# A mixture of softmaxes on one core: units go through TensorE in pairs, and a pair's whole rows are stored at once

## The chip, the core and the metric

The kernel runs on one core of one Trainium2 chip. The metric is the time of one execution on the device in microseconds (us). Before the change it is 789.89 us, the median of three runs (789.84 to 789.98). From here on a time is in us unless it is marked ns, and MB in the working means 1,048,576 bytes where a DMA of 1 MB or 4 MB is meant (the profile's own byte counts are in millions).

## The reference

For each of 32 x 128 = 4096 rows there are four heads with 4096 logits each, and four prior values. The result is a mixture of the four softmaxes, weighed by the softmax of the prior:

```python
prior_probs = softmax(prior, axis=-1)        # (32, 128, 4)
softmax     = softmax(logits, axis=-1)       # (32, 128, 4, 4096)
mixture     = np.sum(prior_probs[..., None] * softmax, axis=2)   # (32, 128, 4096)
```

All of it is float32. The logits are 268 MB, the result is 67 MB; each is moved once.

## The kernel before

**Units and slots.** The 4096 rows make 32 groups `g` of 128 rows, a group is two halves `j` (every second row), and one half with its four heads is a *unit*: 64 rows x 4 heads x 4096 values, 4 MB. There are N = 64 units. A unit lies on 128 partitions as (row m, q): partition 2m + q holds two heads of row m (`i` = 0, 1), 16 KB each, so 32 KB per partition. Five such buffers (`slots`) go round. `load` (L66 to L72) is one DMA of 4 MB on SyncE's queue, and the load of a later unit is issued when the last matmul that reads the slot's present unit is done.

**A unit's work.** For each of the two heads `i` of a partition, `top(n, i)` (L74) takes the negated maximum on VectorE (one 128 x 4096 reduction, L76) and the exponential in place on ScalarE, which also leaves the sum (L79). `weigh(n, i)` (L83) takes the reciprocal of the sum on VectorE (L84), builds a 128 x 64 weight matrix on GpSimd (L86: the selection matrix `sel` times the reciprocal times the prior's share), and issues eight matmuls on TensorE (L93). They sum over the 128 partitions, so that out of (m, q) come 64 rows. The array is used as two column tiles of 64: tile c = 0 makes the columns 0 to 2047 of the 64 rows on PSUM partitions 0 to 63, tile c = 1 the columns 2048 to 4095 on partitions 64 to 127, both with the same weights. The pass with i = 0 starts the sums, the pass with i = 1 adds to them.

**PSUM and the way out.** A unit fills one of two accumulators `accs` (128 x 2048 float32, four banks each), in turn. `evict(n)` (L113) is one ScalarE copy of 128 x 2048 from PSUM to `obuf`, in which group g has one of two halves of 16 KB per partition. When both units of a group are there, `store(g)` (L115) issues two DMAs of 1 MB on ScalarE's queue (L101): one from partitions 0 to 63, one from partitions 64 to 127, each with 8 KB runs, half a row each.

**Order.** The order is written out by hand. In iteration n (w = n - 1 is the unit before) the engines get: `top(n, 0)`; `weigh(w, 1)`, then the load that takes over w's slot; `top(n, 1)`; `weigh(n, 0)`; `evict(w)`; and the store, if w ends a group. So VectorE takes the reciprocal of `weigh(w, 1)` only after the first reduction of unit n, and ScalarE copies w out only after both exponentials of unit n. An engine runs its instructions in this order, and so a waiting instruction holds up what stands behind it.

**End.** The stores of the groups from `HOLD` = 26 to 29 (units 52 to 59, 8 MB) are held back until all loads are issued, so that TensorE, VectorE and ScalarE can finish the last units beside them. Groups 26 and 27 wait in `obuf`, groups 28 and 29 in slot 4, which is no longer loaded, and groups 30 and 31 go to another free slot. The last unit is loaded, copied out and stored in halves.

Of the kernel before, what the change touches and what calls it, by code (L numbers as in the profile page):

```python
# [9 lines left out]
ALU = mybir.AluOpType  # L10
# [3 lines left out]
M = 64  # L14
J = 2
Q = 2
BANK = 512
SLOTS = 5


@with_exitstack
def kernel(
    ctx: ExitStack,
    tc: tile.TileContext,
    logits: bass.AP,
    prior: bass.AP,
    out: bass.AP,
):
    nc = tc.nc
    B, S, H, V = logits.shape  # L30
    R = M * J
    G = B * S // R
    N = G * J
    W = V // 2
    assert G * R == B * S and G == 32 and H == 2 * Q and V == 8 * BANK


    lg = logits.rearrange("b s h v -> (b s) h v").rearrange(
        "(g m j) (q i) v -> g j m q (i v)", m=M, j=J, i=Q
    )  # L40
    ov = out.rearrange("b s v -> (b s) v").rearrange("(g m j) v -> g m j v", m=M, j=J)
    pv = prior.rearrange("b s h -> (b s) h").rearrange("(g r) h -> g r h", r=R)

    cpool = ctx.enter_context(tc.tile_pool(name="cpool", bufs=1))
    psum = ctx.enter_context(tc.tile_pool(name="psum", bufs=1, space=bass.MemoryType.PSUM))

    slots = [cpool.tile([P, Q, V], FP32, name=f"slot{i}") for i in range(SLOTS)]

    obuf = cpool.tile([P, J, V], FP32, name="obuf")
    accs = [psum.tile([P, W], FP32, name=f"acc{i}") for i in range(2)]  # L50

    sel = cpool.tile([P, M], FP32, name="sel")
    wts = [[cpool.tile([P, M], FP32, name=f"wt{k}{i}") for i in range(Q)] for k in range(2)]
    pr = cpool.tile([G, R, H], FP32, name="pr")
    pn = cpool.tile([G, J, Q, M, Q], FP32, name="pn")
    pmax = cpool.tile([G, R], FP32, name="pmax")
    pp = cpool.tile([P, J, Q, G], FP32, name="pp")
    nmax = [cpool.tile([P, N], FP32, name=f"nmax{i}") for i in range(Q)]
    dsum = [cpool.tile([P, N], FP32, name=f"dsum{i}") for i in range(Q)]
    rden = [cpool.tile([P, N], FP32, name=f"rden{i}") for i in range(Q)]  # L60


    def slot(n):
        return slots[n % SLOTS if n < N - 5 else (n - N + 5) % 4]

    def load(n):  # L66
        src = lg[n // J, n % J]
        for i in range(0, Q, Q if n < N - 1 else 1):
            k = Q if n < N - 1 else 1
            nc.sync.dma_start(  # L70
                out=slot(n)[:, i : i + k], in_=src[:, :, i * V : (i + k) * V]
            )  # L72

    def top(n, i):  # L74
        x = slot(n)[:, i]
        nc.vector.tensor_reduce(  # L76
            out=nmax[i][:, n : n + 1], in_=x, axis=AX.X, op=ALU.max, negate=True
        )
        nc.scalar.activation(  # L79
            x, x, AF.Exp, bias=nmax[i][:, n : n + 1], accum_out=dsum[i][:, n : n + 1]  # L80
        )

    def weigh(n, i):  # L83
        nc.vector.reciprocal(rden[i][:, n : n + 1], dsum[i][:, n : n + 1])  # L84
        wt = wts[n % 2][i]
        nc.gpsimd.tensor_scalar(  # L86
            out=wt, in0=sel, scalar1=rden[i][:, n : n + 1],
            scalar2=pp[:, n % J, i, n // J : n // J + 1], op0=ALU.mult, op1=ALU.mult,
        )

        for b in range(W // BANK):
            for c in range(2):
                nc.tensor.matmul(  # L93
                    accs[n % 2][c * M : (c + 1) * M, b * BANK : (b + 1) * BANK],
                    lhsT=wt,
                    rhs=slot(n)[:, i, c * W + b * BANK : c * W + (b + 1) * BANK],
                    start=i == 0, stop=i == Q - 1,
                )

    def part(eng, g, c, js=slice(0, J), lo=0, hi=W):  # L100
        eng.dma_start(  # L101
            out=ov[g, :, js, c * W + lo : c * W + hi],
            in_=home(g)[c * M : (c + 1) * M, js, lo:hi],
        )

    HOLD = G - 6

    def home(g):
        x = obuf if g < G - 4 else slots[4] if g < G - 2 else slot(N - 4)
        return x[:, g % 2].rearrange("p (j w) -> p j w", j=J)  # L110

    def evict(n, lo=0, hi=W):
        nc.scalar.copy(home(n // J)[:, n % J, lo:hi], accs[n % 2][:, lo:hi])  # L113

    def store(g):  # L115
        for c in range(2):
            part(nc.scalar, g, c)

    def prior_user(n):
        return max(k for k in range(n) if slot(k) is slot(n))  # L120

    with tc.manual_schedule():
        for n in range(SLOTS):
            load(n)
        nc.scalar.dma_start(out=pr, in_=pv)

        nc.gpsimd.memset(sel, 1.0)  # L127
        nc.gpsimd.affine_select(  # L128
            out=sel, in_=sel, compare_op=ALU.is_ge, fill=0.0, base=0,
            pattern=[[-Q, M]], channel_multiplier=1,  # L130
        )
        nc.gpsimd.affine_select(  # L132
            out=sel, in_=sel, compare_op=ALU.is_ge, fill=0.0, base=Q - 1,
            pattern=[[Q, M]], channel_multiplier=-1,
        )

        nc.vector.reduce_max(pmax, pr, axis=AX.X)  # L137
        nc.vector.tensor_sub(pr, pr, pmax.unsqueeze(2).to_broadcast([G, R, H]))  # L138
        nc.scalar.activation(pr, pr, AF.Exp)  # L139
        nc.vector.reduce_sum(pmax, pr, axis=AX.X)  # L140
        nc.vector.reciprocal(pmax, pmax)  # L141
        prv = pr.rearrange("g (m j) (q i) -> g j i m q", j=J, i=Q)
        pmv = pmax.rearrange("g (m j) -> g j m", j=J)
        for j in range(J):
            for i in range(Q):
                nc.vector.tensor_mul(  # L146
                    pn[:, j, i], prv[:, j, i], pmv[:, j].unsqueeze(2).to_broadcast([G, M, Q])
                )
        pq = pn.rearrange("g j i m q -> g j i (m q)")
        for t in range(P // 32):  # L150
            nc.vector.transpose(  # L151
                pp[32 * t : 32 * (t + 1)], pq[:, :, :, 32 * t : 32 * (t + 1)]
            )

        for n in range(N):
            w = n - 1
            top(n, 0)
            if n == N - 2:
                for g in range(HOLD, G - 2):
                    part(nc.scalar, g, 1)  # L160
            if w >= 0:
                weigh(w, 1)
                for k in range(SLOTS, N):
                    if prior_user(k) == w:
                        load(k)
                if w == N - 3:
                    for g in range(HOLD, G - 2):
                        part(nc.sync, g, 0)
            top(n, 1)
            weigh(n, 0)  # L170
            if w >= 0:
                evict(w)
                g = w // J
                if w % J == J - 1 and g < HOLD:
                    store(g)
                elif w == N - 3 or w == N - 2:
                    js = slice(0, J) if w == N - 3 else slice(0, 1)
                    part(nc.sync, g, 0, js)
                    part(nc.scalar, g, 1, js)

        n = N - 1
        weigh(n, 1)
        for lo in (0, W // 2):
            evict(n, lo, lo + W // 2)
            part(nc.sync, n // J, 0, slice(1, 2), lo, lo + W // 2)
            part(nc.scalar, n // J, 1, slice(1, 2), lo, lo + W // 2)
# [30 lines left out]
```

## Time and profile before

| what | value |
|---|---|
| median of three runs | 789.89 |
| the profiled execution | 789.42 |
| its span | 787.7 |
| time around the span | 1.7 |
| busy: VectorE / ScalarE / TensorE matmul / GpSimd | 573.4 / 599.8 / 539.4 / 51.1 |
| VectorE reductions, 128 of 128 x 4096 | 4410 ns each |
| ScalarE exponentials, 128 of 128 x 4096 | 3708 ns each, and 187 ns to read the sum |
| ScalarE copies out of PSUM, 56 of 128 x 2048 to `obuf` | 1844 ns each |
| mean granted TensorE clock | 0.88 |

A busy share below 80% on every engine says that none of them sets the time by its sum alone. The matmul row is the time in which at least one matmul was in the array, and it grows when the clock is granted at half rate. The page's lines about the DMA engines, and the order in which units land, are shown with the prediction.

### The profile page before, as it was taken

Reading aid. Unit: us, or ns where it says so; the run is one execution under the profiler, and the core shown is the slowest. Engines: PE = TensorE matmul, PEld = TensorE weight load, DVE = VectorE, ACT = ScalarE, POOL = GpSimd, SP = SyncE. Lnnn points to the kernel's source line nnn. Section 1 sums busy time; section 2 is a strip of 40 time slices with the busy share of each in tenths; the row PEclk is TensorE's granted clock in tenths of the full one; section 3 lists DMA queues with packets and bytes.
Section 4 is the critical chain, followed back from the end, with each engine's and each line's share of the span. In section 5 each row is a group of like instructions: output and inputs, shape, how many; then the busy total and the mean of one; then the engine's idle time right before and its main releaser. Section 6 shows DMA issues by size and latency. Waiting matters only on the chain.

```text
span 787.7 us, 5429 instructions
## 1 busy us (share of the span) xinstructions
PE 539.4 (68%) x2048; PEld 157.7 (20%) x2048; DVE 573.4 (73%) x268; ACT 599.8 (76%) x323; POOL 51.1 (6%) x135
## 2 busy tenths in 40 slices
PE   0777677576677766876767677776687676877772
PEld 0222122121122111221212122211122121222220
DVE  5985867768668677686685866867768678699970
ACT  1897777787787877877878678787787787889991
POOL 0000000000000000000000000000000000000000
PEclk9999897998879998879988887999877998799997
DMA  9999999999999999999999999999999999999998
GB/s 376 438 426 433 433 427 433 431 433 429 433 431 431 431 428 434 429 432 433 433 431 431 434 424 431 433 428 430 431 433 437 429 432 435 431 437 428 424 417 312
DMA packets 18841, 335.95 MB, mean 427 GB/s; under 512 B 2144, under 2 KB 2144, under 8 KB 2432
## 3 DMA queue, kind: packets, MB, share of 16 engines
q1 hardware_dynamic: 10320, 274.73, 81.1%
q10 hardware_dynamic: 8496, 60.89, 18.6%
q8 instruction: 16, 0.26, 0.1%
q14 instruction: 9, 0.07, 0.0%
HBM read 268.50 MB, written 67.11 MB: 426 GB/s over the span
## 4 chain that ended last, share of the span: by engine, by line
DMA 73%; PE 11%; DVE 10%; ACT 2%; issue 1%; POOL 1%; ACTq 0%; SPq 0%; POOLq 0%
DMA slot<-in_logits_dram 73%; PE acc L93 11%; DVE nmax L76 10%; ACT slot L79 1%; POOL wt L86 1%; ACT slot L113 0%; ACTq L101 0%; ACT obuf L113 0%; DVE rden L84 0%; SPq L70 0%; POOLq L86 0%; ACTq L79 0%
## 5 line engine op out<-in xcount | busy, mean ns | idle before, releaser
L93 PE MATMUL acc<-slot,wt 128*64 128x512 f32 x2048 | 539.4, 684 | 233.8 <-POOL wt L86 233.8
L76 DVE TENSOR_REDUCE nmax<-slot 128x1 f32<-128x4096 f32 x128 | 563.5, 4410 | 184.6 <-DMA slot<-in_logits_dram 184.4
L79 ACT ACTIVATE slot<-slot,nmax 128x4096 f32<-128x4096 f32 x128 | 474.7, 3708 | 168.4 <-DVE nmax L76 164.9
L93 PEld LDWEIGHTS acc<-slot,wt 128*64 128x64 f32 x2048 | 157.7, 156 | 614.6 <-POOL wt L86 313.8
L113 ACT COPY obuf<-acc 128x2048 f32<-128x2048 f32 x56 | 103.3, 1844 | 0.0
L86 POOL TENSOR_SCALAR wt<-sel,rden,pp 128x64 f32<-128x64 f32 x128 | 50.3, 393 | 716.2 <-DVE rden L84 716.2
L84 DVE RECIPROCAL rden<-dsum 128x1 f32<-128x1 f32 x128 | 19.6, 153 | 5.9 <-ACT slot L79 5.9
L79 ACT ACTIVATION_READ_ACCUMULATOR slot<-slot,nmax 128x1 f32 x128 | 23.9, 187 | 0.0
L113 ACT COPY slot<-acc 128x2048 f32<-128x2048 f32 (+1 forms) x9 | 14.9, 1658 | 4.8 <-PE acc L93 4.2
L137 DVE TENSOR_REDUCE pmax<-pr 32x128 f32<-32x512 f32 x1 | 0.7, 673 | 2.7 <-DMA pr<-in_prior_dram 2.7
L139 ACT ACT_TABLE_LOAD x1 | 1.3, 1283 | 1.2 <-PEq L201 1.2
L139 ACT ACTIVATE pr<-pr 32x512 f32<-32x512 f32 x1 | 0.6, 628 | 1.6 <-DVE pr L138 1.6
L151 DVE STREAM_TRANSPOSE pp<-pn 32x128 f32<-32x128 f32 x4 | 1.2, 302 | 0.1
L140 DVE TENSOR_REDUCE pmax<-pr 32x128 f32<-32x512 f32 x1 | 0.7, 674 | 0.7 <-ACT pr L139 0.7
L141 DVE RECIPROCAL pmax<-pmax 32x128 f32<-32x128 f32 x1 | 0.9, 941 | 0.0
L146 DVE TENSOR_TENSOR pn<-pr,pmax 32x128 f32<-32x128 f32 x4 | 0.9, 274 | 0.0
L138 DVE TENSOR_TENSOR pr<-pr,pmax 32x512 f32<-32x512 f32 x1 | 0.7, 678 | 0.0
L128 POOL TENSOR_SCALAR_AFFINE_SELECT sel<-sel 128x64 f32<-128x64 f32 x1 | 0.2, 238 | 0.1
L132 POOL TENSOR_SCALAR_AFFINE_SELECT sel<-sel 128x64 f32<-128x64 f32 x1 | 0.2, 238 | 0.1
L127 POOL MEMSET sel<- 128x64 f32 x1 | 0.2, 152 | 0.3 <-POOLq L201 0.3
L201 POOL MEMSET const-float32-0.0<- 128x1 f32 x1 | 0.1, 98 | 0.3 <-issue 0.3
L201 POOL MEMSET const-bfloat16-1.0<- 128x1 bf16 x1 | 0.1, 101 | 0.0
(2 smaller groups left out, 0.2 us busy)
## 6 DMA issues: line engine op xcount, KB each, us to landing
slot<-in_logits_dram SPq DMA_DIRECT2D x63, 4096.0 KB, 38.0
out_dram<-obuf ACTq DMA_DIRECT2D x54, 1024.0 KB, 21.9
slot<-in_logits_dram SPq DMA_DIRECT2D x2, 2048.0 KB, 20.9
out_dram<-slot SPq DMA_DIRECT2D x3, 1024.0 KB, 21.5
out_dram<-slot ACTq DMA_DIRECT2D x3, 1024.0 KB, 21.2
out_dram<-obuf SPq DMA_DIRECT2D x2, 1024.0 KB, 27.5
out_dram<-slot SPq DMA_DIRECT2D x1, 512.0 KB, 15.2
out_dram<-slot ACTq DMA_DIRECT2D x1, 512.0 KB, 13.9
```

The source lines that it names most:

```text
L76: nc.vector.tensor_reduce(out=nmax[i][:, n : n + 1], in_=x, axis=AX.X, op=ALU.max, negate=True)
L79: nc.scalar.activation(x, x, AF.Exp, bias=nmax[i][:, n : n + 1], accum_out=dsum[i][:, n : n + 1])
L84: nc.vector.reciprocal(rden[i][:, n : n + 1], dsum[i][:, n : n + 1])
L86: nc.gpsimd.tensor_scalar(out=wt, in0=sel, scalar1=rden[i][:, n : n + 1], scalar2=pp[:, n % J, i, n // J : n // J + 1], op0=ALU.mult, op1= ...
L93: nc.tensor.matmul(accs[n % 2][c * M : (c + 1) * M, b * BANK : (b + 1) * BANK], lhsT=wt, rhs=slot(n)[:, i, c * W + b * BANK : c * W + (b + ...
L113: nc.scalar.copy(home(n // J)[:, n % J, lo:hi], accs[n % 2][:, lo:hi])
L137: nc.vector.reduce_max(pmax, pr, axis=AX.X)
L138: nc.vector.tensor_sub(pr, pr, pmax.unsqueeze(2).to_broadcast([G, R, H]))
L139: nc.scalar.activation(pr, pr, AF.Exp)
L141: nc.vector.reciprocal(pmax, pmax)
L146: nc.vector.tensor_mul(pn[:, j, i], prv[:, j, i], pmv[:, j].unsqueeze(2).to_broadcast([G, M, Q]))
L151: nc.vector.transpose(pp[32 * t : 32 * (t + 1)], pq[:, :, :, 32 * t : 32 * (t + 1)])
```

## The change

The first 56 units now go in 28 pairs, the last eight units singly as before.

- **Another order of the units.** `place` maps unit n < 56 to group 2 * (n // 4) + n % 2 and half n % 4 // 2. The pair k is the units u = 2k and v = 2k + 1: the same half of two neighbouring groups.
- **Two units in the array at once.** `pair_pass(k, i)` issues 16 matmuls: column tile c = 0 works for u, tile c = 1 for v, each with its own weights, and each goes over all 4096 columns. So both accumulators belong to one pair: `accs[0]` gets columns 0 to 2047, `accs[1]` columns 2048 to 4095, with u's rows on partitions 0 to 63 and v's rows on 64 to 127.
- **Copy and store by pair.** `pair_evict` is two copies of 128 x 2048, after which each partition of `obuf[:, k % 2]` holds a whole row of 16 KB. `store` is one DMA of 2 MB from all 128 partitions.
- **Order.** Per pair: `top(u,0)`; weights (v of the pair before, 1); `pair_pass(k-1, 1)`; both loads into the slots of the pair before; `top(u,1)`; weights (u,0); `pair_evict(k-1)` and its store; `top(v,0)`; weights (u,1); `top(v,1)`; weights (v,0); `pair_pass(k, 0)`.
- **End.** Held back until the loads are issued are the store of the last pair (2 MB, on SyncE's queue) and groups 28 and 29 (4 MB), 6 MB in all. The units 56 to 63 are handled as before.

The core of the diff:

```diff
+    TAIL = N - 8
+
+    def place(n):
+        if n < TAIL:
+            return 2 * (n // 4) + n % 2, n % 4 // 2
+        return n // J, n % J
...
+    def pair_pass(k, i):
+        for b in range(V // BANK):
+            for c in range(2):
+                acc = accs[b // 4][c * M : (c + 1) * M, b % 4 * BANK : (b % 4 + 1) * BANK]
+                matmul(2 * k + c, i, acc, b * BANK)
...
+    def pair_evict(k):
+        for h in range(2):
+            nc.scalar.copy(obuf[:, k % J, h * W : (h + 1) * W], accs[h])
+
+    def store(eng, k):
+        eng.dma_start(
+            out=ov[k // J * J : k // J * J + J, :, k % J].rearrange("g m v -> (g m) v"),
+            in_=obuf[:, k % J],
+        )
...
-    HOLD = G - 6
...
+        for k in range(K):
+            u, v = 2 * k, 2 * k + 1
+            top(u, 0)
+            if k:
+                weight(u - 1, 1)
+                pair_pass(k - 1, 1)
+                reload(u - 2)
+                reload(u - 1)
+            top(u, 1)
+            weight(u, 0)
+            if k:
+                pair_evict(k - 1)
+                store(nc.scalar, k - 1)
+            top(v, 0)
+            weight(u, 1)
+            top(v, 1)
+            weight(v, 0)
+            pair_pass(k, 0)
...
+            if w == N - 3:
+                store(nc.sync, K - 1)
+                for g in (G - 4, G - 3):
+                    part(nc.sync, g, 0)
```

`weight` is the part of `weigh` up to the weight matrix, `unit_pass(n, i)` its eight matmuls, and `reload(n)` issues the load that takes over n's slot.

## The prediction

> **What bounds the kernel now.** I read first the DMA part of the page, then the timeline of VectorE (when units land), then the timeline of one chain through ScalarE, GpSimd and TensorE, then the windows of the end.
>
> ```profile
> span 787.7 us, 5429 instructions
> DMA  9999999999999999999999999999999999999998
> q1 hardware_dynamic: 10320, 274.73, 81.1%
> q10 hardware_dynamic: 8496, 60.89, 18.6%
> HBM read 268.50 MB, written 67.11 MB: 426 GB/s over the span
> ```
>
> The 16 DMA engines are busy in every slice: the two queues together have 99.7% of their time. No compute engine is above 76%. So the time is bytes over the DMA rate. Next, when VectorE can start on a landed unit:
>
> ```profile
> 394.30 4.42 DVE L76 TENSOR_REDUCE nmax<-slot 128x1 f32<-128x4096 f32 x1 [3.26 <-DMA slot<-in_logits_dram]
> 406.43 4.42 DVE L76 TENSOR_REDUCE nmax<-slot 128x1 f32<-128x4096 f32 x1 [3.26 <-DMA slot<-in_logits_dram]
> ...
> 705.91 4.42 DVE L76 TENSOR_REDUCE nmax<-slot 128x1 f32<-128x4096 f32 x1 [0.83 <-DMA slot<-in_logits_dram]
> 715.62 4.42 DVE L76 TENSOR_REDUCE nmax<-slot 128x1 f32<-128x4096 f32 x1 [0.83 <-DMA slot<-in_logits_dram]
> ```
>
> In the middle a unit lands every 12.13, and in that time 4 MB come in and 1 MB goes out. Near the end, where the stores are held, a unit lands every 9.71. So a load costs 9.71 / 4 = 2.43 per MB, and a store 12.13 - 9.71 = 2.42 per MB. This is the row that decides about the stores.
>
> **The change part by part.**
>
> *Stores: 56 of 1 MB with 8 KB runs from 64 partitions become 28 of 2 MB with 16 KB runs from 128.* The bytes stay. What a larger run saves is bounded from two sides. By the queues' shares: q1 takes 0.811 x 787.7 x 16 / 274.73 = 37.2 engine-us per million bytes, q10 0.186 x 787.7 x 16 / 60.89 = 38.5. If the stores of the pairs (28 x 2.1 = 58.7 million bytes) fell to q1's price, 58.7 x 1.3 / 16 = 4.7 us would go. By the landings: a store's MB already costs what a load's MB costs, with runs of 32 KB, and nothing is left to gain; a loss is excluded by the same row, since runs of 8 and of 32 KB cost alike and 16 lies between. I take 0, because the landings measure what the chain waits for, while packet times overlap and q10's share holds the slow stores of the end.
>
> [...]
>
> *Two units share the accumulators.* Before, TensorE went on with the next unit in the other accumulator; now `pair_pass(k, 0)` needs both copied out. This closes a ring: pass 1 of a pair ends, ScalarE copies the second accumulator, issues the store, does the first exponential of v, VectorE and GpSimd make the weights, pass 0 of the next pair starts. The end of the trace has just this sequence:
>
> ```profile
> 757.30 1.84 ACT L113 COPY slot<-acc 128x2048 f32<-128x2048 f32 x1
> 759.17 0.54 ACTq L101 DMA_DIRECT2D out_dram<-slot  x1
> 759.76 3.71 ACT L79 ACTIVATE slot<-slot,nmax 128x4096 f32<-128x4096 f32 x1 [0.61 <-ACT slot L113]
> 763.59 0.16 DVE L84 RECIPROCAL rden<-dsum 128x1 f32<-128x1 f32 x1 [1.26 <-ACT slot L79]
> 763.95 0.39 POOL L86 TENSOR_SCALAR wt<-sel,rden,pp 128x64 f32<-128x64 f32 x1 [5.35 <-DVE rden L84]
> 764.40 8.76 PE L93 MATMUL acc<-slot,wt 128*64 128x512 f32 x32 [2.09 <-POOL wt L86]
> ```
>
> From copy to first matmul 764.40 - 757.30 = 7.10. The pair's passes are twice 32 matmul instructions. At full clock 16 take 3.65:
>
> ```profile
> 705.73 3.65 PE L93 MATMUL acc<-slot,wt 128*64 128x512 f32 x16 [0.73 <-POOL wt L86]
> ```
>
> After an idle time the clock is granted at half for a while: the 32 above took 8.76, not 7.30. A gap of 7 us will always bring that once a pair: 8.76 + 7.30 = 16.1. The ring is 7.10 + 16.1 = 23.2. A pair's DMA time is 2 x 12.13 = 24.26. The ring fits, by 1.1. This assumes that the first accumulator, complete after half of pass 1, is copied beside the other half; ScalarE is free then.
>
> *In step with the landings* (u lands at 0): pass 1 of the pair before can start at 5.1 (first reduction, reciprocal, weights, as from 394.30 in the trace). Pass 0 starts 9.5 after v's landing (second reduction, reciprocal, weights), at 12.1 + 9.5 = 21.6, runs to 30.4 and is in front of pass 1 of its own pair (ready at 24.3 + 5.1 = 29.4), which ends at 37.7, that is 13.4 after the next u. ScalarE has both exponentials of u done at 12.8, so the copies run 12.8 to 16.5 and wait for nothing; the store's issue ends at 17.1. Queued behind them are the exponentials of v, ready at 16.6, so 0.5 late; VectorE needs the first one's sum only after v's second reduction, at 21.0, and it is there then. Sums per pair: VectorE 4 x (4.41 + 0.15) = 18.2, ScalarE 4 x 3.9 + 3.7 + 0.6 = 19.9, TensorE 16.1. All fit in 24.26: cost 0. ScalarE issues one store per pair in place of two (saves 0.6 of an engine that isn't the bound).
>
> *Loads leave later, two at a time.* Before:
>
> ```profile
> slot<-in_logits_dram SPq DMA_DIRECT2D x63, 4096.0 KB, 38.0
> out_dram<-obuf ACTq DMA_DIRECT2D x54, 1024.0 KB, 21.9
> ```
>
> A load is in the queue for 38, three units deep. Now, when u lands, two slots hold the pair before, one holds u, and two loads are outstanding, the last due at 24.3. The next two are issued at 13.4. So 10.9 of work is still queued: cost 0. The loads' median from issue to landing should fall to about 29 (23 and 35 in turn).
>
> *Start.* The first release moves. Pass 0 of pair 0 starts where the second unit's first matmuls did, at 32.8, and takes 8.8; pass 1 another 7.3: loads 5 and 6 are issued at 48.8, not at 32.3 and 41.8. Units land every 9.7 at first, the fifth at 42.8 + 9.7 = 52.5. The queue is nearly empty then, with some 2 us left after the fixed latency of a load (the first landed at 13.7, of which 9.7 is transfer). Then the ring gains 1.1 a pair, and the queue fills. Cost 0, up to 2.5 where the cold clock lasts longer.
>
> *End.* 6 MB are held back, not 8 MB. So 2 MB of stores move out of the stage of pure stores, which is slow (369, 385, 342 GB/s in windows of 2 us from 774 on), into the mixed one at 432. 2.1 million bytes at 370 are 5.7, at 432 they are 4.85: 0.8 gained. The landing of unit 62 moves from 744.7 to about 749.5; its last copies and stores are issued 32 later as before, at 781.8, and their 1 MB is done near 785. The other 9 MB, from the last landing at about 758 and at some 400 GB/s, last to 782: the cover just holds. If it is gone, up to 2 us appear.
>
> **Sum.** 0 + 0 + 0 - 0.8 against the profiled execution's 789.42 (span 787.7 and 1.7 around it): 788.6. The median of the runs lies 0.47 above that execution, so I forecast 789.1 for the median.
>
> **The rivals.** A difference of 0.2% (1.6 us) is about what a measurement of this kernel can tell from no change.
>
> *B, faster:* larger runs do pay, by the queues' shares. Half of 4.7 and the 0.8 of the end: -3.1, 786.8. For it: q10's share. Against it: 2.42 beside 2.43 per MB.
>
> *C, slower, the ring becomes the bound.* If the copy of the first accumulator waits for all of pass 1, the ring is 23.2 + 1.84 = 25.0, above 24.26: 0.8 a pair over 27 pairs, 20, less 3 that the queue gives at first: 806. It decides from 17.2 of TensorE per pair on (24.26 - 7.10). For it: the very last copy, of half an accumulator, started only when all of its unit's matmuls were done (773.21). Against it: those were halves of one accumulator, and here there are two. Worse still, if two column tiles with different weights don't run side by side (the change doesn't do what it says), a pass doubles, and some 365 us come on top; 2048 weight loads for 2048 matmuls say that each tile already loads its own. That is 1 in 100, and I count it here.
>
> *D, slower, the queue runs dry at the start, or the cover at the end is too short:* +2.5 to +3.5, 792.4. The point is 50.5 for the issue of load 5, or an end of the 9 MB ahead of 782.
>
> **Chances.** Forecast (A) 0.50; B 0.21; C 0.15; D 0.14. So faster by over 0.2% 0.21, within 0.50, slower 0.29. The range takes in A (788.3 to 791.4), nearly all of B, and D: 786.5 to 794; left out are C, and the far end of B, together under 0.2.
>
> **What would show it.** Right: units still land 24.26 apart by pairs, the DMA row stays at 9 throughout, the loads' median from issue to landing falls to about 29, the TensorE clock is at half once a pair, and the end of the loads is some 5 later while the span ends at about the same time. Wrong: VectorE waits for DMA between pairs by more than before and the DMA row shows 8 in the middle (C); a gap of the DMA near 50 or 780 (D); pairs that land clearly less than 24.2 apart (B).

## The result, and the profile after

| | before | after |
|---|---|---|
| median of eight runs each | 789.74 (789.34 to 789.98) | 792.16 (791.73 to 792.65) |
| ratio | | 1.0031 [1.0021, 1.0042] |
| the profiled execution, its span | 789.42, 787.7 | 791.84, 790.1 |
| unit 62 lands | 744.75 | 749.38 |
| from there to the end of the span | 42.95 | 40.7 |

The changed kernel is slower by 2.4, or 0.31%, where a gain of 0.8 was forecast (789.1). The time lies inside the stated range, but by luck: the range reached that far for rival D, whose mechanism did not occur (see below). Two executions in the slow state (one of 814.22 in e5, one of the kernel before beside it) are left out of every time and ratio here.

A landing is read as the start of the first reduction that waited for the load. For unit 62, first before, then after:

```profile
744.75 4.42 DVE L76 TENSOR_REDUCE nmax<-slot 128x1 f32<-128x4096 f32 x1 [0.83 <-DMA slot<-in_logits_dram]
749.38 4.42 DVE L89 TENSOR_REDUCE nmax<-slot 128x1 f32<-128x4096 f32 x1 [0.83 <-DMA slot<-in_logits_dram]
```

The page of the kernel after, the lines that answer to those of before:

```profile
span 790.1 us, 5387 instructions
DMA  9999999999999999999999999999999999999998
GB/s 375 438 411 429 445 423 433 429 438 432 434 431 431 426 435 434 433 433 430 433 431 432 430 431 431 428 440 430 430 434 428 435 431 425 440 430 434 423 390 280
q1 hardware_dynamic: 10176, 274.73, 81.2%
q10 hardware_dynamic: 4608, 60.89, 18.3%
HBM read 268.50 MB, written 67.11 MB: 425 GB/s over the span
```

The DMA row stays at 9, as before. It shows only tenths of a slice of some 20 us, but no slice points to an idle DMA; bytes that move more slowly while the engines count as busy are the likelier loss. The GB/s row says where: 423 to 445 from the fourth slice to the 38th, then 390 and 280 in the last two slices. Before, the last two had 417 and 312.

Next the windows of the stage in which only stores are left, 4 us each. The columns are the stretch and its length, the busy time of TensorE's matmuls and weight loads, VectorE, ScalarE and GpSimd, the granted TensorE clock, the DMA share and GB/s. First before:

```profile
765.00:769.00 4.00, 4.00 (x14) 1.12 (x12) 0.16 (x1) 4.00 (x3) 0.39 (x1) 0.65 1.02 393
769.00:773.00 4.00, 4.00 (x20) 1.12 (x16) 0.00 (x0) 0.00 (x1) 0.00 (x0) 1.00 1.01 395
773.00:777.00 4.00, 0.16 (x2) 0.00 (x0) 0.00 (x0) 2.02 (x2) 0.00 (x0) 1.00 1.02 377
777.00:781.00 4.00, 0.00 (x0) 0.00 (x0) 0.00 (x0) 0.00 (x0) 0.00 (x0) 0.63 1.01 352
```

The same stretches after:

```profile
765.00:769.00 4.00, 1.94 (x10) 0.43 (x6) 2.12 (x2) 4.00 (x3) 0.33 (x1) 1.00 0.93 301
769.00:773.00 4.00, 3.84 (x18) 1.25 (x20) 0.17 (x1) 4.00 (x3) 0.46 (x2) 1.00 1.00 381
773.00:777.00 4.00, 3.46 (x16) 0.87 (x14) 0.00 (x0) 1.21 (x2) 0.00 (x0) 1.00 1.02 375
777.00:781.00 4.00, 0.00 (x0) 0.00 (x0) 0.00 (x0) 1.54 (x2) 0.00 (x0) 0.73 1.00 286
```

In 765 to 769 and in 777 to 781 the rate is 301 and 286, at a DMA share of 0.93 and 1.00; before, the same stretches had 393 and 352. The share does not follow the rate: it is 1.00 at 286 GB/s as it is 1.01 at 352. This is why the share alone would show nothing here.

One more view, the DMA issues (count, size of one, median us from issue to landing), after:

```profile
slot<-in_logits_dram SPq DMA_DIRECT2D x63, 4096.0 KB, 24.4
out_dram<-obuf ACTq DMA_DIRECT2D x27, 2048.0 KB, 18.7
...
out_dram<-slot SPq DMA_DIRECT2D x3, 1024.0 KB, 35.2
out_dram<-slot ACTq DMA_DIRECT2D x3, 1024.0 KB, 15.1
out_dram<-obuf SPq DMA_DIRECT2D x1, 2048.0 KB, 30.0
```

The 1 MB stores of the end now take 35.2 on SyncE's queue and 15.1 on ScalarE's. Before, the same two rows read 21.5 and 21.2. The two queues have come out of balance, in bytes (4 MB against 2 MB of what is held) and in the partitions: SyncE's queue holds the pair's store from all 128 partitions and the lower halves (partitions 0 to 63), ScalarE's queue only upper halves (64 to 127).

### The profile page after: what moved, and what is told of

The parts are those of the page before. It is cut to its first block, busy times and chain, and to the rows that moved or that the text cites. A ratio compares the mean times of both kernels' runs of the same rounds, so it can differ in the third digit from the quotient of the medians.

```text
span 790.1 us, 5387 instructions
## 1 busy us (share of the span) xinstructions
PE 532.4 (67%) x2048; PEld 160.6 (20%) x2048; DVE 573.6 (73%) x268; ACT 602.8 (76%) x323; POOL 51.2 (6%) x135
## 3 DMA queue, kind: packets, MB, share of 16 engines
q10 hardware_dynamic: 4608, 60.89, 18.3%
## 4 chain that ended last, share of the span: by engine, by line
DMA 47%; PE 26%; DVE 15%; ACT 5%; issue 4%; POOL 1%; ACTq 0%; SPq 0%; POOLq 0%
DMA slot<-in_logits_dram 47%; PE acc L105 26%; DVE nmax L89 15%; ACT slot L92 3%; ACT obuf L126 2%; POOL wt L99 1%; ACT slot L145 0%; DVE rden L98 0%; ACTq L129 0%; ACTq L135 0%; SPq L78 0%; POOLq L99 0%; ACTq L92 0%
## 5 line engine op out<-in xcount | busy, mean ns | idle before, releaser
L105 PE MATMUL acc<-slot,wt 128*64 128x512 f32 x2048 | 532.4, 665 | 244.0 <-POOL wt L99 238.3
L105 PEld LDWEIGHTS acc<-slot,wt 128*64 128x64 f32 x2048 | 160.6, 153 | 614.9 <-issue 338.3
L126 ACT COPY obuf<-acc 128x2048 f32<-128x2048 f32 x56 | 103.2, 1858 | 23.2 <-PE acc L105 23.1
## 6 DMA issues: line engine op xcount, KB each, us to landing
slot<-in_logits_dram SPq DMA_DIRECT2D x63, 4096.0 KB, 24.4
out_dram<-slot SPq DMA_DIRECT2D x3, 1024.0 KB, 35.2
out_dram<-slot ACTq DMA_DIRECT2D x3, 1024.0 KB, 15.1
```

Of the source, the lines that this page charges most:

```text
L105: nc.tensor.matmul(dst, lhsT=wts[n % 2][i], rhs=slot(n)[:, i, lo : lo + BANK], start=i == 0, stop=i == Q - 1,)
L126: nc.scalar.copy(obuf[:, k % J, h * W : (h + 1) * W], accs[h])
```

## The experiments

**The theories.** The first, P in the expectations, is about partitions: when only stores run, one half of the partitions can be read at about half the rate, so the full rate needs both halves read at once in equal amounts. That it is half was the author's assumption; e2 below measures it, with 211, 240 and 219 GB/s where the kernel before had 424, 414 and 377. Before, the halves stood so: lower halves on one queue against upper halves on the other. After, SyncE's queue begins with a store from all partitions, and so the upper half is asked for by both queues, and later as many lower halves are left alone. The rivals: the middle costs something (the pairs' order, or the 2 MB store beside the loads); the ring through the accumulators is late; the cover of the end, 6 MB in place of 8, is too short; the bytes held are unequal (4 MB on SyncE's queue, 2 MB on ScalarE's). The last one alone is not enough to slow the bytes: from 741 to 756 the kernel after has nearly all its DMA traffic (loads) on SyncE's queue and runs at 422 GB/s, and e2 below is slow with equal bytes on both queues. That it adds something beside the halves is not excluded. In the expectations, Q stands for the short cover and R for the middle.

One thing these runs do not part: in a 1 MB store of a single group, the half of the partitions also decides which half of each output row is written. So "half" below means both together; that it is the partitions, and not the place in the output, is the author's assumption, and no run here shows it apart.

Every ratio below is to the kernel before in the same session, whose medians were 789.50 to 789.75.

**e1: the last pair's store as two halves, one on each queue.** `half(eng, k, c)` is a 1 MB store of pair k from partitions 0 to 63 (c = 0) or 64 to 127 (c = 1).

```diff
             if n == N - 2:
+                half(nc.scalar, K - 1, 1)
...
             if w == N - 3:
-                store(nc.sync, K - 1)
+                half(nc.sync, K - 1, 0)
```

> The held store of the last pair goes out as two DMAs of 1 MB: partitions 0 to 63 on SyncE's queue, 64 to 127 on ScalarE's, in front of the held half stores of the same partitions. All else as in the changed kernel. Theory P (in the tail the two queues no longer read opposite partition halves: the whole-partition store stands on SyncE's queue against upper-half stores on ScalarE's, and later lower-half stores are left alone, so packets of 8 KB take 450 to 520 ns in place of 310): the 16 engines get back to 370 to 430 GB/s between 761 and 781, and the time falls by 2.5 to 3.5, to about 789. Rival Q (the cover is too short, 6 MB held and not 8): the bytes held and the last copies are the same, so no change, 792. Rival R (pairs cost something in the middle): no change, 792.

Measured: 789.77, ratio 1.0003 [0.9994, 1.0012]. Its windows:

```profile
765.00:769.00 4.00, 2.03 (x10) 0.43 (x6) 2.21 (x2) 4.00 (x3) 0.29 (x1) 1.00 1.03 416
...
777.00:781.00 4.00, 0.00 (x0) 0.00 (x0) 0.00 (x0) 1.57 (x2) 0.00 (x0) 1.00 0.98 342
```

301 has become 416 and 286 has become 342, with the same engine work beside them (ScalarE 4.00 in the first, TensorE 1.94 and 2.03). The edit touches one 2 MB store of the 67 MB, and the whole loss of 2.4 is gone. Unit 62 lands at 749.47, within 0.1 of the kernel after, so what happens earlier has no part in the loss.

**e8: 26 pairs, then twelve single units, the tail as before (8 MB held, all as halves).**

```diff
-    TAIL = N - 8
+    TAIL = N - 12
+    HOLD = G - 6
...
-                store(nc.sync, K - 1)
-                for g in (G - 4, G - 3):
+                for g in range(HOLD, G - 2):
                     part(nc.sync, g, 0)
...
                 pair_evict(K - 1)
+                store(nc.scalar, K - 1)
...
```

The last pair is stored beside loads like the others, and groups 26 and 27 wait in `obuf` as before the change.

> 26 pairs, then twelve single units that are stored and held (8 MB, lower halves on SyncE's queue, upper halves on ScalarE's) as in the kernel before. Only the middle keeps the change. Theory P: the whole loss was in the tail, so the time is that of the kernel before or 0.3 below it, 789.4 to 789.8. Rival Q: same, as 8 MB are held again. Rival R (the middle costs): stays near 792.

Measured: 789.10, ratio 0.9994 [0.9985, 1.0003]. It was run a second time, beside the kernels of another session:

> The kernel with 26 pairs and twelve single units once more, beside the one with 6 MB held on the same chip. It was 0.9994 [0.9985, 1.0003] of the kernel before. If the middle gains what fewer DMAs save (28 of 56 completions, some 0.3), it stays at 0.999 to 1.000.

Measured: 789.09, ratio 0.9994 [0.9985, 1.0003]. So 26 pairs in the middle cost nothing that can be measured. Both intervals include no change, so a gain isn't shown either; the 0.3 that the second expectation puts on fewer DMAs is the author's guess, and no run shows it. The rival "the middle costs something" is out.

**e2: the kernel before, with both queues on the same half.** The held stores are ordered so that both queues read lower halves first and then both upper ones. Bytes, sizes and counts stay.

```diff
             if n == N - 2:
-                for g in range(HOLD, G - 2):
-                    part(nc.scalar, g, 1)
+                for c in range(2):
+                    for g in (G - 4, G - 3):
+                        part(nc.scalar, g, c)
...
-                    for g in range(HOLD, G - 2):
-                        part(nc.sync, g, 0)
+                    for c in range(2):
+                        for g in (HOLD, HOLD + 1):
+                            part(nc.sync, g, c)
```

> The kernel before, with the eight held stores of 1 MB in another order: both queues first store lower halves (SyncE groups 26 and 27, ScalarE groups 28 and 29), then both upper halves. Bytes, sizes, queues and the work of all compute engines stay. Theory P: for some 8 MB all engines read one half of the partitions at a time, at about half the rate (8.4 million bytes at some 220 GB/s in place of 430: up to 19 longer), so 800 to 809. Rivals Q and R (the halves don't matter): no change, 789.8.

Measured: 807.18, ratio 1.0222 [1.0208, 1.0236], 17.7 slower. Its windows:

```profile
757.00:761.00 4.00, 3.27 (x16) 0.91 (x14) 4.00 (x3) 2.15 (x3) 0.39 (x1) 1.00 1.01 211
761.00:765.00 4.00, 1.21 (x6) 0.14 (x2) 1.23 (x1) 2.90 (x1) 0.00 (x0) 1.00 0.99 240
...
773.00:777.00 4.00, 3.61 (x18) 0.98 (x14) 0.00 (x0) 0.34 (x1) 0.00 (x0) 1.00 0.99 219
```

211 to 240 GB/s with the DMA engines 0.99 to 1.01 busy; before, these stretches had 424, 414 and 377. The mean of the three is 223. By it the 8.39 million bytes held would take 37.6 in place of 21.0 at 400, an estimate of +16.6 beside the 17.7 measured. The other windows up to 793 lie between 218 and 291; by the mean of all nine from 757 on, 239, the estimate is +14.1. This isolates the mechanism in the old kernel, without any pair.

**e4: the pairs' stores in the middle as two 1 MB halves on ScalarE's queue.** The kernel after, with its end unchanged.

```diff
-                store(nc.scalar, k - 1)
+                half(nc.scalar, k - 1, 0)
+                half(nc.scalar, k - 1, 1)
```

> The changed kernel, but in the middle each pair's store goes out as two DMAs of 1 MB, from partitions 0 to 63 and 64 to 127, both on ScalarE's queue, with the same 16 KB runs. Theory P: beside loads the stores read SBUF for a third of the time at most, and two engines on one half seldom meet; the middle stays at 24.26 per pair and the time within 0.5 of the changed kernel, 791.7 to 792.7. If reading from all partitions does pay in the middle, a pair takes longer, by up to 2.4 per MB: 800 and more.

Measured: 792.89, 0.2 above what was expected, ratio 1.0039 [1.0024, 1.0054], beside 1.0031 [1.0021, 1.0042] for the kernel after. All partitions in one store, or one half after the other: beside loads it makes no difference that can be measured. ScalarE's queue, which carries these stores, has 18.3% of the DMA engines' time on the page of the kernel after, below the expectation's third; that two engines seldom meet on one half is the expectation's own reason, and no view shows it. The runs are of 16 KB in both, so this says nothing about their size; e8 does, in which the middle has 16 KB runs and the kernel before 8 KB. By the two together, the larger stores, the substance of the change, neither gain nor lose in the middle.

**e5: the pair's store behind the half stores on SyncE's queue.**

```diff
             if w == N - 3:
-                store(nc.sync, K - 1)
                 for g in (G - 4, G - 3):
                     part(nc.sync, g, 0)
+                store(nc.sync, K - 1)
```

> The changed kernel with one line moved: on SyncE's queue the lower-half stores of groups 28 and 29 stand ahead of the held whole-partition store, not behind it. Theory P: lower halves now meet upper halves (4 MB at some 400 GB/s and more), and only the whole-partition store meets the upper halves of the last groups, so a part of the 2.5 comes back: 789.8 to 791.2. If only splitting the store helps, and not what it stands against: 792.

Measured: 791.9, ratio 1.0029 [1.0017, 1.0040], above what was expected. Its windows say why:

```profile
757.00:761.00 4.00, 3.27 (x16) 0.92 (x14) 4.00 (x3) 3.60 (x3) 0.39 (x1) 1.00 0.99 416
...
769.00:773.00 4.00, 3.75 (x18) 1.15 (x20) 0.16 (x1) 4.00 (x3) 0.55 (x2) 1.00 0.98 340
773.00:777.00 4.00, 3.56 (x16) 0.97 (x16) 0.00 (x0) 1.21 (x2) 0.00 (x0) 1.00 0.99 317
777.00:781.00 4.00, 0.00 (x0) 0.00 (x0) 0.00 (x0) 1.63 (x2) 0.00 (x0) 1.00 1.00 304
```

While lower halves stand against upper ones, 416; from the point where the whole store stands against upper halves, 340 and 317, and 304 in the window in which it runs out. The loss has moved later and is not gone. The likely reason, which the expectation had missed: the surplus of one half is the same wherever the whole store stands.

**e3: two whole stores against each other.** Pair 26 is held too and goes whole on ScalarE's queue, pair 27 whole on SyncE's; 8 MB are held.

```diff
-                store(nc.scalar, k - 1)
+                if k < K - 1:
+                    store(nc.scalar, k - 1)
...
             if n == N - 2:
+                store(nc.scalar, K - 2)
```

> The changed kernel with two pairs held (8 MB in all): pair 26 goes out whole on ScalarE's queue, pair 27 whole on SyncE's, each ahead of the half stores. Theory P: no queue is left with one half, and whole stores don't meet on a half; from that 788.8 to 789.2. But the last pair then has no store beside its loads, its DMA time is 19.4, and the ring through PSUM, 23.8 in the trace, is longer: ScalarE may end some 4 behind and take back up to 2, so 789 to 791. Rival Q (only the bytes held count): 789.7 and below.

Measured: 789.99, ratio 1.0007 [0.9998, 1.0016]. The window in which both whole stores run:

```profile
757.00:761.00 4.00, 3.27 (x18) 0.96 (x16) 4.00 (x3) 3.35 (x4) 0.40 (x1) 1.00 1.03 442
```

So a whole store is not slow in itself: 442 beside another whole one, and 414 and 410 in the windows before and behind. What costs is its standing against a queue of one half.

**e10: one half store out of place in the kernel before.** The upper half of group 26 moves from ScalarE's queue to the front of SyncE's held stores.

```diff
-                for g in range(HOLD, G - 2):
+                for g in range(HOLD + 1, G - 2):
                     part(nc.scalar, g, 1)
...
+                    part(nc.sync, HOLD, 1)
                     for g in range(HOLD, G - 2):
                         part(nc.sync, g, 0)
```

> The kernel before, with one held store of 1 MB (the upper half of group 26) moved from ScalarE's queue to the front of the held ones on SyncE's, so that SyncE's queue holds 5 MB and ScalarE's 3. Nothing else changes, no pairs. Theory P: upper halves meet upper halves for 1 MB each, and as many lower halves are left alone at the end, about as in the changed kernel: 2 to 5 slower, 791.7 to 794.7. Rivals: a queue's share of the bytes doesn't matter, 789.7.

Measured: 797.35, ratio 1.0095 [1.0081, 1.0110], 7.6 slower; the direction was right and the size too small. The expectation counted too little: 1 MB out of place makes 2 MB in which upper meets upper (264 GB/s in 757 to 761, before 424) and later 2 MB of lower halves with no partner. With e2's 223, an estimate for each of these is 2.1 x (1/223 - 1/400) x 1000 = 4.2, together 8.4, beside the 7.6 measured.

**e6: the two copies of a pair in the other order.** Now the copy that needs the end of the pass comes first, and the first accumulator waits behind it. This tests the ring.

```diff
     def pair_evict(k):
-        for h in range(2):
+        for h in (1, 0):
```

> The changed kernel with the two copies of a pair in the other order: the accumulator that is complete last is copied first, so the other copy (1.87) can no longer run beside the second half of the pass. The ring through PSUM, 23.8 from the first matmul of one pair to that of the next in the trace's first pairs, becomes some 25.6 and passes the pair's DMA time of 24.26. If the ring decides from there on: 27 pairs x 1.3 to 1.4, 35 less up to 8 of lead, so 815 to 828, with idle DMA engines in the middle. If the ring has more room than I think, or the order of the copies doesn't matter: 792.

Measured: 805.44, ratio 1.0207 [1.0192, 1.0221]. The mechanism came as expected, at a smaller size. One turn of the ring in its timeline:

```profile
404.91 15.59 PE L105 MATMUL acc<-slot,wt 128*64 128x512 f32 x62 [3.95 <-POOL wt L99]
...
420.54 3.63 ACT L126 COPY obuf<-acc 128x2048 f32<-128x2048 f32 x2 [3.71 <-PE acc L105]
...
429.26 15.36 PE L105 MATMUL acc<-slot,wt 128*64 128x512 f32 x62 [3.95 <-POOL wt L99]
```

Both copies follow the whole pass (404.91 + 15.59 = 420.50), and the pairs start 429.26 - 404.91 = 24.35 apart here and 594.84 / 24 = 24.8 apart on average, above the 24.26 of the DMA. The chain that ended last now goes through TensorE for 58% of the span and through loads for 5%; in the kernel after it is 26% and 47%. The kernel after stays below 24.26 by this overlap alone. The idle DMA engines that were expected do not show: from 50 to 700 the share is 1.00 in both kernels, and only the rate differs, 424 GB/s here and 432 in the kernel after.

**e9 and e12: e8 with less held.** e9 holds 6 MB in place of 8 (group 26 is stored when it is copied out), e12 holds 4 MB (groups 26 and 27 are).

```diff
-    HOLD = G - 6
+    HOLD = G - 5
...
+            if w == 2 * HOLD - 1:
+                part(nc.scalar, HOLD - 1, 0)
+                part(nc.scalar, HOLD - 1, 1)
```

> The kernel with 26 pairs and twelve single units, but group 26 is stored when its second unit is copied out, so that 6 MB are held back in place of 8, in balanced halves. It asks about the cover alone. Rival Q (part of the loss comes from the shorter cover): 0.5 to 2 slower than with 8 MB held, 789.6 to 791. Theory P alone (only halves count): the same as with 8 MB or up to 0.8 faster, since 2 MB leave the stage of pure stores: 788.3 to 789.2.

Measured: 788.78, ratio 0.9987 [0.9978, 0.9996], below both kernels. With balanced halves 6 MB cover the end: the DMA share is 1.03 and 0.97 in the windows 769 to 773 and 777 to 781. So the rival "the cover of 6 MB is too short" is out; e1, which also holds 6 MB, agrees.

> 26 pairs, then twelve single units, and only groups 28 and 29 (4 MB) held back. Each 2 MB that leave the stage of pure stores (some 385 GB/s) for the mixed one (432) save some 0.6; the last copies come 4.9 later for each 2 MB. With 6 MB held it was 0.9987 of the kernel before. If the cover still holds: 788.0 to 788.6. If it is now too short: 789.5 to 793.

Measured: 792.68, ratio 1.0041 [1.0027, 1.0055]. Here the cover does fail:

```profile
773.00:777.00 4.00, 3.57 (x16) 1.06 (x16) 0.16 (x1) 4.00 (x3) 0.70 (x2) 1.00 0.95 344
777.00:781.00 4.00, 3.73 (x18) 1.06 (x16) 0.00 (x0) 1.21 (x2) 0.07 (x1) 1.00 0.66 172
```

A cover that is too short shows in the DMA share (0.66) while TensorE still works (3.73 of 4). The kernel after has a share of 0.93 to 1.00 at its low rates. In these two ends the column tells the two kinds of loss apart. It doesn't always: e6 lost its time to a wait at a share of 1.00.

**e13: the kernel before with 6 MB held.**

```diff
-    HOLD = G - 6
+    HOLD = G - 5
```

> The kernel before with one number changed: 6 MB held back in place of 8. No pairs. If the gain of the version with 26 pairs and 6 MB held comes from holding less, this has it too: 788.8 to 789.3. If it comes from the pairs: 789.5 to 790.

Measured: 789.14, ratio 0.9993 [0.9985, 1.0002]. The interval includes no change, so a gain from holding less is not shown without pairs, and it overlaps e9's. What e9 owes to holding less and what to the pairs stays open.

## Why the prediction was wrong, point by point

*Stores, 0: right in the middle, not in the stage of pure stores.* The row 2.42 per MB is a row of stores beside loads, and e4 shows that there the partitions of a store don't matter (ratio 1.0039 beside 1.0031). But "a loss is excluded by the same row" was carried over to the stage of pure stores, where no row stood for it. The one hint was that the stage was slower (369, 385, 342 in the prediction's windows), and that was not asked further. With stores alone, e2 with both queues on one half ran at 211, 240 and 219 GB/s in the windows shown, up to 291 in the others. Beside loads no run here shows such a loss: stores are a fifth of the bytes there, and 1 MB per 12.13 is only 86 GB/s on average.

*The ring, fits by 1.1: right that it fits, with less room.* The first matmuls of the first pairs, on the timeline of the kernel after:

```profile
32.94 16.51 PE L105 MATMUL acc<-slot,wt 128*64 128x512 f32 x64 [7.70 <-POOL wt L99]
...
56.48 16.69 PE L105 MATMUL acc<-slot,wt 128*64 128x512 f32 x64 [7.03 <-POOL wt L99]
...
80.15 16.80 PE L105 MATMUL acc<-slot,wt 128*64 128x512 f32 x64 [6.99 <-POOL wt L99]
```

The starts are 23.54 and 23.67 apart (predicted 23.2), the passes of a pair take 16.5 to 16.8 (predicted 16.1), and the gap is 7.0 (predicted 7.1). Until 175 the starts drift to 23.89 apart, with passes of 16.9, so the room is 0.4 and not 1.1; from 200 on the passes take up to 17.6, and the starts are about 24.3 apart, as the landings are. The half clock that the prediction put at the head of a pass shows there: 0.50 from 764.40 to 767.50 before, and 0.51 from 418 to 424 in the kernel after, twice as long; the pass that starts at 418.01 took 17.57. The assumption on which rival C turned, that the first accumulator is copied beside the second half of the pass, holds: in that pass the first copy starts at 432.59, and the second waits for TensorE until 434.87. And e6 shows what its failure costs, 13 to 14 more than the kernel after (C said 17).

*Loads two at a time, and the start, 0: right in the cost.* Loads 5 and 6 are issued at 48.69 and 49.53 (predicted 48.8). The loads' median falls from 38.0 to 24.4, 5 below the predicted 29, and yet the landings keep their pace: from unit 8 to unit 50 they take 511.3, before 510.95, so two units land 511.3 / 21 = 24.35 apart, before 24.33.

*End, -0.8: this is the step that failed.* It measured +2.4. The prediction priced the 9 MB behind the last load at "some 400 GB/s", whatever the two queues read; two of the windows ran at 301 and 286. The landing of unit 62 came as the prediction put it (749.38 against 749.5), so from there 37.4 were forecast (749.5 to 787.7 - 0.8 = 786.9) and 40.7 measured. The prediction feared for the cover, as rival D; its 792.4 meets the time, but its mechanism did not occur, since the DMA share stays at 0.93 and above where D needs a gap, and e1 is without the loss under the same cover. What took place is the unbalanced halves: with one store split (e1) the loss is gone. Its size is only estimated. From 757 to 761 SyncE's queue, with runs of 16 KB, moved 1.13 of 1.64 million bytes, about two of three; by that division 2 MB of the upper half and 1 MB of the lower are read by the time it is through, and 1 MB of lower halves is left alone later. By e2's 223 and by 400 otherwise that is an estimate of (2.1 / 223 - 3.15 / 400) x 1000 = 1.5 and (1.05 / 223 - 1.05 / 400) x 1000 = 2.1, together 3.6, beside the 3.3 found against the forecast. The agreement is rough: the windows 757 to 761 and 761 to 765 still ran at 410 and 395, with the stores of both queues under way. In bytes, without that estimate: from 761 to 781 the kernel after moves 6.95 million (395, 301, 381, 375 and 286 over 4 us each), e1 7.64 million (393, 416, 393, 365, 342). The 0.69 million that are missing take 2.1 at the 330 GB/s of the next window, nearly all of the 2.4.

*The 0.8 for holding less* is not settled. With 6 MB held in balanced halves, e9 measures 1.0 below before, e13 0.4 below and e1 0.3 above, each with an interval of about 0.7 to either side; only e9's excludes no change.

*Rival B* (786.8, larger runs pay) is out by e8, which has 16 KB runs in the middle and the old end: its interval ends at 0.9985, 1.2 below before, where B needs 2.3 for the runs (half of 4.7; the rest of its 3.1 is the end).

What stays open: e1 and e9 have the same landing of unit 62 and the same 6 MB held, and e9 is 1.2 lower, each against before. They differ in what is held (a pair's halves with 16 KB runs, or single groups) and in the last units' order; no run parts these.

## What to carry to other kernels

A cost per byte read from the mixed stage of this kernel did not hold in the stage where stores run alone: 2.42 per MB beside loads, and an estimated 4.7 from e2's 223 GB/s (2.6 from 400). Where a change alters the shape of a transfer, price each stage by a row of that stage. With stores alone, what ran fastest here were opposite halves of the partitions in equal amounts on the two queues (424 GB/s from 757 to 761 before), or whole-partition stores on both (442, e3); one whole 2 MB store against a queue of one half cost 2.4. And when GB/s fall at a full DMA share, look at what the transfers read as well as for a wait: the share stood at 1.00 in both cases here (e2, e6).

## What of the hardware was not expected

- With stores alone, both queues on one half ran at 211 to 291 GB/s (e2, 757 to 793), opposite halves at 352 to 424 (the kernel before, 757 to 781), and whole against whole at 410 to 442 (e3, 753 to 765). A whole store against upper halves ran at 410, 395 and 301 in turn (the kernel after, 757 to 769) and at 340 and 317 (e5). Beside loads, whole or half made no difference (e4).
- The DMA share was 1.01 at 211 GB/s (e2) as at 424 (the kernel before), both from 757 to 761.
- A pair's passes with a gap of about 7 ahead of them take 16.5 to 17.6; the granted TensorE clock was 0.77 to 0.79 from 50 to 200, before 0.86 to 0.90, and it cost nothing that shows in the landings, since the ring still fitted.
